# Attention, index and scan heads two at a time on the two halves of the matmul array, their GpSimd work on VectorE, and modulation sums in two column halves

## Chip, core and metric

The kernel runs on one core of one Trainium2 chip. The metric is the device time of one execution in microseconds (us). TensorE (PE) multiplies; its array has 128 rows (the partitions that are contracted) and 128 columns (the partitions of the result in PSUM). VectorE (DVE), ScalarE (ACT) and GpSimd (POOL) do the element-wise work, and SyncE (SP) issues most transfers. Every engine works through its own queue in order.

## What is computed

The program is two transformer-like blocks on 512 tokens of width 1024. The change touches the first block's mixer: an attention that keeps the best 128 keys of each query by an index score, a state-space scan in chunks of 128 tokens, and the modulation vectors.

```python
mod = cond @ w_ada + b_ada                       # six vectors of 1024
sh_m, sc_m, g_m, sh_f, sc_f, g_f = jnp.split(mod, 6)
h = _rms(x, norm_mix) * (1 + sc_m) + sh_m
q, kv_lat, q_i, k_i, w_i, z, xbc, dt_raw, gate_logits = _split(h @ w_in)
# index, per query q, 8 heads of 64
dots = jnp.einsum('bqhd,bsd->bqhs', q_i, k_i)
score = jnp.einsum('bqh,bqhs->bqs', w_i, jax.nn.relu(dots))   # causal; top 128 kept
# attention, 8 heads of 64
logits = q . k * scale + bias(dist);  p = softmax(logits);  y = p @ v
# scan, 16 heads of 64, state 128, chunks of 128
wmat = cb[..., None] * lmat * dtc
y = wmat @ xc + (cc @ state) * exp(acum)
state = state * exp(acum[-1]) + (decay * xc)^T @ bc
```

After it come the mixer's output products, a mixture of 32 experts (about 400 MB of weights), and the second block. None of these is touched.

## The kernel before

The mixer has one long stream of large products: `proj` (from L524) takes a group of 256 columns of `w_in`, splits the weights into a high part H (`nc.scalar.copy`, L368) and a low part L (a subtraction, L370: seven of eight on VectorE, one on GpSimd), and multiplies three times per block (`mm3`, L387 to L389, 512 columns each). There are 2 groups for the queries, the key and value products, and then 18 groups in `ssm`.

Everything else of the mixer is written as Python generators. After each step of `proj` the function `pace` advances two lists by the rates of the tables `RATES` and `R0`: `bg` (index `scores`, then `qknorm`, `steps`, `heads`, and `ssd` once its inputs are there) and `bg2` (`topk` for three query blocks, then `modrest`, the four modulation vectors that are needed late). So small matmuls stand between large ones in PE's queue; what is left when the groups end is drained.

- `scores` (L628): for a query block t (1 to 3) and each of 8 heads one matmul that contracts 64 rows, then ReLU on ACT and a weighted sum on DVE.
- `heads` (L780 to L859): 32 units, one for a query block t (0 to 3) and a head h. `weights` multiplies q and k of the head (L813, 64 rows: the lower half of the array for even heads, the upper for odd, up to 512 columns), adds mask and bias and takes the maximum on DVE (L817, L819), takes exp on ACT (L824), and normalises on DVE (L826, L827). `turn` transposes the result, block by block (L835), and ACT copies it (L837). `output` multiplies with v (L847, 64 columns of the array, the half given by the head; t + 1 matmuls). In step i the unit i is weighed, i - 1 turned and i - 2 multiplied. `bias` (L796, 8 calls) is on GpSimd.
- `ssd` (L1172 to L1281): four chunks. `weights` prepares four heads at a time (L1212, L1215 on DVE, exp on ACT, and the product L1221 on GpSimd); `output` multiplies, head by head, L1234 and (from the second chunk) L1236, both in the column half of the head; `post` scales on GpSimd (L1253, L1258) and updates the state (L1261).
- `modrest` (L1303 to L1338): sums eight weighted rows on DVE (L1318), then one matmul with a single column of ones per half of 512 (L1324), a copy, a DMA, and for two of the vectors four tiny matmuls per half (L1336).

float32 operands pass through the array twice, so each such matmul is two records in the trace ("x2" is one matmul of a head); the transposes are one. PSUM tiles come from two rings of four banks, "mm" for large products and "at" for the rest.

Of the kernel before, what the change touches and what calls it, by code (L numbers as in the profile page):

```python
# [18 lines left out]
P = 128  # L19
# [143 lines left out]
R0 = (2.5, 1), (3, 0.75), (2, 1.25)  # L163
RATES = ([1.35, 1.35, 1.125, 1.125, 1.125, 1.125, 1.125, 1.125, 1.35, 1.125, 1.125, 1.125, 1.125, 1.125, 1.125, 0.9, 0.9, 0.45],
# [102 lines left out]
class Kern:  # L267
# [352 lines left out]
    def scores(self, qiT, kiT, wi):  # L620
        nc, c = self.nc, self.c
        for t in range(1, NT):
            n = (t + 1) * P
            sc = self.pt([P, n], f"score{t}")
            for h in range(8):
                r0 = 64 * (h % 2)
                b = self.bank()
                nc.tensor.matmul(b[:, :n], lhsT=qiT[r0:r0 + 64, h // 2, t * P:(t + 1) * P], rhs=kiT[r0:r0 + 64, :n], start=True, stop=True)  # L628
                rl = self.w2()
                nc.scalar.activation(rl[:, :n], b[:, :n], AF.Relu)  # L630
                if h == 0:
                    nc.vector.tensor_scalar(sc, rl[:, :n], wi[:, t, :1], 0.0, op0=OP.mult, op1=OP.add)
                else:
                    nc.vector.scalar_tensor_tensor(sc, rl[:, :n], wi[:, t, h:h + 1], sc, op0=OP.mult, op1=OP.add)
                if h == 7:
# [144 lines left out]
    def heads(self):  # L780

        nc, c = self.nc, self.c
        qT, kT, V, T = self.qT, self.kT, self.V, self.T
        units = [(t, h) for t in range(NT) for h in range(8)]
# [7 lines left out]
        def bias(t, hq):  # L792
# [3 lines left out]
            nc.gpsimd.tensor_tensor(mb[:, :, :near], T[:, 4 * hq:4 * hq + 4, 256 - near:],  # L796
# [3 lines left out]
        def weights(t, h):  # L800
# [3 lines left out]
            if h % 4 == 0:  # L804
                nt, nq = (t, 1) if h == 0 else (t + 1, 0)
                if (t, h // 4) not in mbs:
                    bias(t, h // 4)
                if nt < NT:
                    bias(nt, nq)
            mb = mbs[t, h // 4]  # L810
            r0 = 64 * (h % 2)
            b = self.bank()
            nc.tensor.matmul(b[:, :n], lhsT=qT[r0:r0 + 64, h // 2, t * P:n], rhs=kT[r0:r0 + 64, h // 2, :n], start=True, stop=True)  # L813
            lg = self.w2()
            mx = self.small([P, 2])
            if far:
                nc.vector.tensor_tensor_reduce(out=lg[:, :far], in0=b[:, :far], in1=mask(t)[:, :far], scale=1.0,  # L817
                                               scalar=-3.0e38, op0=OP.add, op1=OP.max, accum_out=mx[:, 1:])
            nc.vector.tensor_tensor_reduce(out=lg[:, far:n], in0=b[:, far:n], in1=mb[:, h % 4, :near], scale=1.0,  # L819
                                           scalar=mx[:, 1:] if far else -3.0e38, op0=OP.add, op1=OP.max, accum_out=mx[:, :1])  # L820
            nm = self.small([P, 1])
            nc.vector.tensor_scalar(nm, mx[:, :1], -1.0, None, op0=OP.mult)
            ss = self.small([P, 1])
            nc.scalar.activation(lg[:, :n], lg[:, :n], AF.Exp, bias=nm, accum_out=ss)  # L824
            rs = self.small([P, 1])
            nc.vector.reciprocal(rs, ss)  # L826
            nc.vector.tensor_scalar(lg[:, :n], lg[:, :n], rs, None, op0=OP.mult)  # L827
            st[t, h] = lg

        def turn(t, h):  # L830
            n = (t + 1) * P
            lg = st[t, h]
            pb = self.bank()
            for k in range(t + 1):
                nc.tensor.transpose(pb[:, k * P:(k + 1) * P], lg[:, k * P:(k + 1) * P], c("ident"))  # L835
            pt = self.w2()
            nc.scalar.copy(pt[:, :n], pb[:, :n])  # L837
            st[t, h] = pt

        def output(t, h):  # L840
            pt = st.pop((t, h))
            if h % 2 == 0:
                st["y"] = self.bank()
            yb = st["y"]
            r0 = 64 * (h % 2)
            for k in range(t + 1):
                nc.tensor.matmul(yb[r0:r0 + 64, :P], lhsT=V[:, k, h * 64:(h + 1) * 64], rhs=pt[:, k * P:(k + 1) * P], start=k == 0, stop=k == t)  # L847
            if h % 2:
                nc.scalar.copy(self.yat[:, h // 2, t * P:(t + 1) * P], yb[:, :P])

        for i in range(len(units) + 2):
# [3 lines left out]
            if 0 < i <= len(units):  # L855
# [316 lines left out]
    def ssd(self):  # L1172
# [31 lines left out]
        def weights(ch, hq):  # L1204
# [12 lines left out]
            if ch:  # L1217
# [3 lines left out]
                nc.gpsimd.tensor_tensor(e3, e3, BC[:, 2 + g, None, cs].to_broadcast([P, 4, P]), op=OP.mult)  # L1221
# [4 lines left out]
        def output(ch, hq):  # L1226
# [4 lines left out]
            for h in range(4):  # L1231
                o = yb[64 * (h % 2):64 * (h % 2) + 64, (h // 2) * P:(h // 2 + 1) * P]
                H = hq * 4 + h
                nc.tensor.matmul(o, lhsT=xdt[:, H], rhs=w[:, h * P:(h + 1) * P], start=True, stop=ch == 0)  # L1234
# [1227 lines left out]
```

## Time and profile before

| | |
|---|---|
| median of 3 runs | 2329.55 us (2326.49 to 2334.56) |
| profiled execution, its own time | 2326.67 us |
| its span, first to last instruction | 2324.9 us |
| PE busy | 2199.6 us (95%) |
| VectorE busy | 1518.0 us (65%) |
| ScalarE busy | 982.2 us (42%) |
| GpSimd busy | 291.5 us (13%) |
| granted TensorE clock | 0.981 |

Shares over the span mix stages with different limits. The mixer's products with the work between them lie from about 60 to 490 us; experts follow to about 1640 us, and the second block after that. A record's printed length for PE is modelled; what a matmul costs is read from the distance of the starts around it.

### The profile page before, as it was taken

The page shows a single profiled execution, that of the slowest core. Times are in us where ns is not written, and L with a number is a line of the kernel's source. Part 1 is how long each engine was busy: PE and PEld are TensorE (multiplying, and loading weights), DVE is VectorE, ACT ScalarE, POOL GpSimd, SP SyncE. Part 2 cuts the span into 40 slices and gives each one's busy share as a digit, 9 for nine tenths or more (in the row PEclk, how much of TensorE's full clock was granted, in tenths as well). Part 3 has the DMA queues.
Part 4 walks back from the last instruction along what each step waited for, and adds up shares of the span by engine and source line. Part 5 has one row for each costly group of instructions (what it writes and reads, how often), then busy time and mean ns, then how long its engine had stood idle before and what let it go on. Part 6 is the DMA issues. An engine that isn't in the chain of part 4 may idle for free. (4 is left out here: it accounts for less than half of the span.)

```text
span 2324.9 us, 28001 instructions
## 1 busy us (share of the span) xinstructions
PE 2199.6 (95%) x10209; PEld 1576.0 (68%) x10209; DVE 1518.0 (65%) x2480; ACT 982.2 (42%) x1375; POOL 291.5 (13%) x173
## 2 busy tenths in 40 slices
PE   6999999999899999999999999999799999999898
PEld 4676667678666657655656666666368888888676
DVE  7678878864776668766667667776442534458864
ACT  4424443432444446534345445544233422336642
POOL 2011101421111100110010010000000111002110
PEclk9999999999899999999999999999989999999999
DMA  8323344652889999999999999999732222132221
GB/s 313 99 94 107 122 150 173 231 205 115 313 339 398 407 405 411 398 411 397 395 397 398 397 397 379 405 404 408 300 110 91 91 91 91 73 109 87 77 91 37
DMA packets 93938, 576.36 MB, mean 248 GB/s; under 512 B 12591, under 2 KB 14361, under 8 KB 32611
## 3 DMA queue, kind: packets, MB, share of 16 engines
q1 hardware_dynamic: 79856, 540.60, 59.4%
q0 software_dynamic: 8432, 18.21, 3.1%
q10 hardware_dynamic: 5508, 15.71, 1.8%
q8 instruction: 82, 1.34, 0.2%
q14 instruction: 60, 0.49, 0.1%
HBM read 556.74 MB, written 27.59 MB: 251 GB/s over the span
## 5 line engine op out<-in xcount | busy, mean ns | idle before, releaser
L370 DVE TENSOR_TENSOR L<-raw,H 128x1024 fp32r<-128x1024 f32 x476 | 582.5, 1257 | 258.1 <-ACT H L368 245.8
L368 ACT CAST H<-raw 128x1024 fp32r<-128x1024 f32 x496 | 508.8, 1051 | 473.8 <-DMA raw<-in_w_dn_dram 148.0
L388 PE MATMUL mm<-L,hl 128*128 128x512 f32 x536 | 211.2, 394 | 5.1 <-DVE L L370 5.1
L387 PE MATMUL mm<-H,hl 128*128 128x512 f32 x536 | 211.5, 395 | 1.3 <-ACT H L368 1.3
L389 PE MATMUL mm<-H,hl 128*128 128x512 f32 x536 | 209.5, 391 | 0.0
L387 PE MATMUL mm<-U,H 128*128 128x512 f32 (+1 forms) x488 | 187.6, 384 | 3.0 <-DVE U L710 3.0
L389 PE MATMUL mm<-U,L 128*128 128x512 f32 (+1 forms) x488 | 185.2, 381 | 1.1 <-POOL L L370 1.1
L388 PE MATMUL mm<-U,H 128*128 128x512 f32 (+1 forms) x488 | 186.2, 382 | 0.0
L1674 PE MATMUL mm<-raw,sx 128*64 128x512 f32 x792 | 179.3, 598 | 0.0
L387 PE MATMUL mm<-E,H 128*128 128x512 f32 x416 | 172.8, 418 | 3.9 <-ACT E L393 3.9
L387 PE MATMUL mm<-H,U 128*128 128x512 f32 x424 | 169.8, 401 | 2.1 <-DVE w L2361 2.0
L389 PE MATMUL mm<-H,U 128*128 128x512 f32 x424 | 167.8, 396 | 0.0
L388 PE MATMUL mm<-E,H 128*128 128x512 f32 x416 | 165.7, 398 | 1.6 <-DVE E L394 1.6
L388 PE MATMUL mm<-L,U 128*128 128x512 f32 x424 | 167.1, 394 | 0.0
L389 PE MATMUL mm<-E,L 128*128 128x512 f32 x416 | 165.2, 397 | 0.0
L388 PE MATMUL at<-L,hl 128*128 128x512 f32 x272 | 111.1, 408 | 18.8 <-DVE L L370 18.7
L388 PEld LDWEIGHTS mm<-L,hl 128*128 128x128 f32 x536 | 100.7, 188 | 32.2 <-DVE L L370 12.1
L1674 PEld LDWEIGHTS mm<-raw,sx 128*64 128x64 f32 x792 | 53.9, 137 | 98.5 <-issue 92.7
L387 PE MATMUL at<-H,hl 128*128 128x512 f32 x272 | 108.8, 400 | 11.5 <-ACT H L368 11.5
L387 PEld LDWEIGHTS mm<-H,hl 128*128 128x128 f32 x536 | 100.9, 188 | 22.7 <-ACT H L368 1.7
L389 PEld LDWEIGHTS mm<-H,hl 128*128 128x128 f32 x536 | 100.6, 188 | 20.8
L387 PEld LDWEIGHTS mm<-U,H 128*128 128x128 f32 x488 | 92.7, 190 | 22.1 <-DVE U L710 3.1
(452 smaller groups left out, 3731.4 us busy)
## 6 DMA issues: line engine op xcount, KB each, us to landing
raw<-in_w_gu_dram SPq DMA_DIRECT2D x212, 1024.0 KB
raw<-in_w_dn_dram SPq DMA_DIRECT2D x103, 1024.0 KB
XU<-in_w_gu_dram SPq DMA_DIRECT2D x44, 1024.0 KB
XU<-in_w_dn_dram SPq DMA_DIRECT2D x25, 1024.0 KB
raw<-in_win_dram SPq DMA_DIRECT2D x20, 1024.0 KB
raw<-in_w_ada_dram SPq DMA_DIRECT2D x16, 1024.0 KB
raw<-in_wug_dram SPq DMA_DIRECT2D x16, 1024.0 KB
raw<-in_wxg_dram SPq DMA_DIRECT2D x12, 1024.0 KB
```

The source lines that it names most:

```text
L368: nc.scalar.copy(h[:, :m], src)
L370: eng.tensor_tensor(l[:, :m], src, h[:, :m].bitcast(F32), op=OP.subtract)
L387: t.matmul(out, lhsT=lhs[0], rhs=rhs[0], start=start, stop=False)
L388: t.matmul(out, lhsT=lhs[0], rhs=rhs[1], start=False, stop=False)
L389: t.matmul(out, lhsT=lhs[1], rhs=rhs[0], start=False, stop=stop)
L1674: nc.tensor.matmul(bs[i // 2][64 * (i % 2):64 * (i % 2) + 64], lhsT=x[:, k], rhs=w[:, i * 512:(i + 1) * 512], start=False, stop=k == KD - 1)
```

## The change

1. `scores`, `heads` and `ssd.output` issue two heads' matmuls next to each other: QK of an even and an odd head (row halves), PV alternating between the two heads (column halves), the scan's matmuls alternating. `heads` has 16 units of two heads; `output` now follows the `turn` of the same unit, and `turn` copies back into the tile that it read.
2. 25 element-wise operations move from GpSimd to VectorE: `bias` (8), the scan's product with C (12), and the two scalings in `post` (3 and 2).
3. `modrest` multiplies with 64 columns of ones for each half of 512, one in the lower, one in the upper column half; the tiny matmuls of both halves follow after a yield, in one bank with one copy.
4. `RATES` and `R0` are about halved where heads run in pairs.

```diff
-R0 = (2.5, 1), (3, 0.75), (2, 1.25)
-RATES = ([1.35, 1.35, 1.125, 1.125, 1.125, 1.125, 1.125, 1.125, 1.35, 1.125, ...
+R0 = (1.25, 1), (1.5, 0.75), (1, 1.25)
+RATES = ([1.35, 1.35, 0.7, 0.6, 0.6, 0.6, 0.6, 0.6, 0.65, 0.6, 0.6, 0.6, 0.7, 1.125, ...
...
-            nc.gpsimd.tensor_tensor(mb[:, :, :near], T[:, 4 * hq:4 * hq + 4, 256 - near:],
+            nc.vector.tensor_tensor(mb[:, :, :near], T[:, 4 * hq:4 * hq + 4, 256 - near:],
...
+            bs = [self.bank() for _ in range(2)]
+            for i in range(2):
+                r0 = 64 * i
+                nc.tensor.matmul(bs[i][:, :n], lhsT=qT[r0:r0 + 64, h0 // 2, t * P:n], rhs=kT[r0:r0 + 64, h0 // 2, :n], start=True, stop=True)
...
+            for lg in st[t, h0]:
+                pb = self.bank()
+                for k in range(t + 1):
+                    nc.tensor.transpose(pb[:, k * P:(k + 1) * P], lg[:, k * P:(k + 1) * P], c("ident"))
+                nc.scalar.copy(lg[:, :n], pb[:, :n])
...
+            yb = self.bank()
             for k in range(t + 1):
+                for i, pt in enumerate(pts):
+                    nc.tensor.matmul(yb[64 * i:64 * i + 64, :P], lhsT=V[:, k, (h0 + i) * 64:(h0 + i + 1) * 64], rhs=pt[:, k * P:(k + 1) * P], start=k == 0, stop=k == t)
...
-            if i > 1:
-                output(*units[i - 2])
+                output(*units[i - 1])
                 yield
...
-                nc.gpsimd.tensor_tensor(e3, e3, BC[:, 2 + g, None, cs].to_broadcast([P, 4, P]), op=OP.mult)
+                nc.vector.tensor_tensor(e3, e3, BC[:, 2 + g, None, cs].to_broadcast([P, 4, P]), op=OP.mult)
...
+                for last in (False, True) if ch else (False,):
+                    for i in (h, h + 1):
+                        o = yb[64 * (i % 2):64 * (i % 2) + 64, (i // 2) * P:(i // 2 + 1) * P]
...
-            nc.gpsimd.tensor_tensor(xdt, xdt, dec[:, :, None].to_broadcast([P, 16, 64]), op=OP.mult)
+            nc.vector.tensor_tensor(xdt, xdt, dec[:, :, None].to_broadcast([P, 16, 64]), op=OP.mult)
...
-                nc.gpsimd.tensor_tensor(s3, s3, ea[:, :, None].to_broadcast([P, 16, 64]), op=OP.mult)
+                nc.vector.tensor_tensor(s3, s3, ea[:, :, None].to_broadcast([P, 16, 64]), op=OP.mult)
...
+            b = self.bank()
             for h in range(2):
+                nc.tensor.matmul(b[64 * h:64 * h + 64], lhsT=c("ones")[:, :64], rhs=acc[:, h * 512:(h + 1) * 512], start=True, stop=True)
```

How this stands in the queues, at three places. First PE, in the heads of the last query block, before the change: one head's PV (L847, four matmuls into one column half), six products, the next head's QK (L813). Names are out<-in, the last figure the shape of the result.

```order
L389 MATMUL mm_2584<-E_68,L_2580 128x512
L847 MATMUL at_2686<-w_650_2684,XU_937 64x128 x4
L387 MATMUL mm_2765<-E_67,H_2757 128x512
L388 MATMUL mm_2765<-E_69,H_2757 128x512
L389 MATMUL mm_2765<-E_67,L_2758 128x512
L387 MATMUL mm_2766<-E_67,H_2757 128x512
L388 MATMUL mm_2766<-E_69,H_2757 128x512
L389 MATMUL mm_2766<-E_67,L_2758 128x512
L813 MATMUL at_2773<-U_882,U_578 128x512
L387 MATMUL mm_2765<-E_67,H_2757 128x512
```

The same engine and place after the change, first the QK of two heads (L818), then the transposes of two heads (L845), the products behind them, and PV (L853).

```order
L388 MATMUL mm_2571<-E_69,H_2562 128x512
L389 MATMUL mm_2571<-E_67,L_2563 128x512
L818 MATMUL at_2588<-U_882,U_578 128x512
L818 MATMUL at_2589<-U_882,U_578 128x512
L387 MATMUL mm_2570<-E_67,H_2562 128x512
L388 MATMUL mm_2570<-E_69,H_2562 128x512
L389 MATMUL mm_2570<-E_67,L_2563 128x512
```

The two QK rows stand next to each other, in two banks. A little further on in the same queue come the transposes of the pair before and its PV.

```order
L845 MATMUL at_2630<-cst_66,w_583_2486 128x128 x4
L845 MATMUL at_2636<-cst_66,w_587_2494 128x128 x4
L387 MATMUL mm_2570<-E_68,H_2566 128x512
L388 MATMUL mm_2570<-E_70,H_2566 128x512
L389 MATMUL mm_2570<-E_68,L_2567 128x512
L387 MATMUL mm_2571<-E_68,H_2566 128x512
L388 MATMUL mm_2571<-E_70,H_2566 128x512
L389 MATMUL mm_2571<-E_68,L_2567 128x512
L853 MATMUL at_2648<-w_583_2486,XU_937 64x128
L387 MATMUL mm_2570<-E_68,H_2566 128x512
L853 MATMUL at_2648<-w_587_2494,XU_937 64x128
L853 MATMUL at_2648<-w_583_2486,XU_937 64x128
```

PV alternates between the two heads' tiles, and six products stand between the last transpose and the first PV matmul, where the copy by ACT has to be done. In the whole stream 32 single QK rows have become 16 pairs, and all 16 PV groups alternate. In the index scores the rows stand in the same order as before.

Third place: VectorE in the scan. Before, its queue holds the weights (L1212, L1215), the low parts (L370), the sums of `modrest` (L1318) and the outputs (L1240), while L1221, L1253 and L1258 stand in GpSimd's queue.

```order
L1264 TENSOR_TENSOR state_2942<-state_2942,at_3395 128x512
L1264 TENSOR_TENSOR state_2942<-state_2942,at_3398 128x512
L1215 TENSOR_TENSOR w_795_3443<-w_795_3443,cb_3309 128x512
L1318 SCALAR_TENSOR_TENSOR macc_3095<-raw_3560,cond_84,macc_3095 128x1024
L1240 SCALAR_TENSOR_TENSOR U_990<-U_990,prm_72,at_3426 128x128 x2
L1212 TENSOR_SCALAR w_798_3477<-raw_3174,ac_1305 128x128 x4
L370 TENSOR_TENSOR L_3524<-raw_3517,H_3523 128x1024
L1215 TENSOR_TENSOR w_798_3477<-w_798_3477,cb_3309 128x512
L1240 SCALAR_TENSOR_TENSOR U_990<-U_990,prm_72,at_3460 128x128 x2
L1212 TENSOR_SCALAR w_816_3570<-raw_3407,ac_1305 128x128 x4
L1318 SCALAR_TENSOR_TENSOR macc_3095<-raw_3586,cond_84,macc_3095 128x1024 x2
```

After, the scaling (L1259) and the products with C (L1225) stand between them.

```order
L1216 TENSOR_SCALAR w_706_3099<-raw_2930,ac_1311 128x128 x4
L1227 COPY s_696_3045<-raw_2930 128x4
L1216 TENSOR_SCALAR w_709_3133<-raw_2930,ac_1311 128x128 x3
L1246 SCALAR_TENSOR_TENSOR U_991<-U_991,prm_72,at_3069 128x128 x2
L1259 TENSOR_TENSOR w_669_2892<-w_669_2892,s_702_3087 128x1024
L1219 TENSOR_TENSOR w_706_3099<-w_706_3099,cb_3030 128x512
L1225 TENSOR_TENSOR w_707_3106<-w_707_3106,U_989 128x512
L1216 TENSOR_SCALAR w_709_3133<-raw_2930,ac_1311 128x128
L1225 TENSOR_TENSOR w_710_3140<-w_710_3140,U_989 128x512
L1272 COPY state_2886<-at_3091 128x512
L1272 COPY state_2886<-at_3094 128x512
```

From the output product of the attention onwards (after the groups of `ssm`), every engine's queue is the same as before, row for row.

## Rows read from the trace of the kernel before

**Rows 1.** Windows: us, then busy us (records) of PE, PEld, DVE, ACT, POOL; clock, DMA share, GB/s.

```profile
165.00:340.00 175.00, 173.46 (x755) 117.10 (x754) 135.96 (x317) 71.33 (x156) 24.59 (x11) 1.00 0.36 124
400.00:450.00 50.00, 45.63 (x282) 35.31 (x281) 46.82 (x83) 19.90 (x33) 25.33 (x14) 1.00 0.63 223
700.00:1600.00 900.00, 868.97 (x4000) 557.40 (x3999) 624.18 (x827) 420.32 (x476) 81.90 (x54) 1.00 1.01 400
```

**Rows 2.** Timeline of PE in the heads: start, us, engine, line, operation.

```profile
174.15 0.48 PE L813 MATMUL at<-U,U 64*128 64x128 f32 x2
174.57 0.50 PE L387 MATMUL mm<-E,H 128*128 128x512 f32 x1
...
347.12 1.09 PE L847 MATMUL at<-w,XU 128*64 128x128 f32 x8
348.13 0.50 PE L387 MATMUL mm<-E,H 128*128 128x512 f32 x1
...
349.17 0.39 PE L388 MATMUL mm<-E,H 128*128 128x512 f32 x1
349.40 0.40 PE L389 MATMUL mm<-E,L 128*128 128x512 f32 x1
349.72 1.12 PE L813 MATMUL at<-U,U 64*128 64x512 f32 x2
350.78 0.50 PE L387 MATMUL mm<-E,H 128*128 128x512 f32 x1
```

**Rows 3.** Timeline of PE, index scores: twelve heads and the next product.

```profile
102.65 3.48 PE L628 MATMUL at<-w,U 64*128 64x384 f32 x12
106.33 3.59 PE L628 MATMUL at<-w,U 64*128 64x512 f32 x12 [0.20 <-ACT w L630]
109.85 0.50 PE L388 MATMUL mm<-E,H 128*128 128x512 f32 x1
```

**Rows 4.** Timeline of PE, first chunk of the scan: four heads.

```profile
382.87 0.66 PE L1234 MATMUL at<-w,w 128*64 128x128 f32 x8
383.45 0.50 PE L388 MATMUL mm<-E,H 128*128 128x512 f32 x1
```

**Rows 5.** Timeline of PE, a modulation sum and the next product.

```profile
329.79 1.02 PE L1324 MATMUL at<-macc,cst 128*1 128x512 f32 x2
330.74 0.50 PE L388 MATMUL mm<-E,H 128*128 128x512 f32 x1
```

**Rows 6.** GpSimd's groups, 160 to 470 us: busy, mean ns, idle before.

```profile
L1221 POOL TENSOR_TENSOR w<-w,U 128x512 f32<-128x512 f32 x12 | 18.5, 1554 | 42.0 <-ACT w L1219 42.0
L796 POOL TENSOR_TENSOR w<-XU,score 128x1024 f32<-128x1024 f32 x6 | 15.6, 2614 | 63.9 <-DMA gate<-w 24.0 <-DVE s L819 15.2 <-DVE score L650 13.7
L1253 POOL TENSOR_TENSOR w<-w,s 128x1024 f32<-128x1024 f32 x3 | 6.9, 2312 | 4.0 <-PE at L1236 2.7 <-DVE w L1212 1.3
```

**Rows 7.** VectorE in the scan: groups (busy, mean ns); then by line, ns min/median/max.

```profile
L1212 DVE TENSOR_SCALAR w<-raw,ac 128x128 f32<-128x128 f32 x64 | 24.3, 441 | 1.5 <-PE at L1236 1.5
L1215 DVE TENSOR_TENSOR w<-w,cb 128x512 f32<-128x512 f32 x16 | 14.8, 935 | 0.8 <-ACT w L1213 0.8
...
L1212 DVE TENSOR_SCALAR w<-raw,ac x64: 273/279/1943, 361.1 to 458.1; 128x128 f32<-128x128 f32 x64
L1215 DVE TENSOR_TENSOR w<-w,cb x16: 679/686/1811, 369.6 to 459.4; 128x512 f32<-128x512 f32 x16
L370 DVE TENSOR_TENSOR L<-raw,H x476: 1202/1221/4811, 66.3 to 2289.8; 128x1024 fp32r<-128x1024 f32 x159
```

**Rows 8.** ScalarE's groups, 165 to 470 us: busy, mean ns, idle before.

```profile
L368 ACT CAST H<-raw 128x1024 fp32r<-128x1024 f32 x34 | 35.4, 1046 | 37.2 <-PE mm L388 28.2 <-DMA raw<-in_win_dram 4.9 <-DMA raw<-in_wao_dram 4.1
L837 ACT COPY w<-at 128x512 f32<-128x512 f32 x8 | 4.7, 586 | 15.6 <-PE at L835 13.3 <-DMA raw<-in_w_ada_dram 2.3
```

**Rows 9.** Waits of VectorE and PE: total us, times, longest us.

```profile
DVE s L826 <- ACT w L824: 20.4, 19, 3.1
...
PE at L1261 <- ACT bt L1249: 3.4, 1, 3.4
```

More of the change, by code (lines that the diff above doesn't have):

```diff
@@ L783, in heads @@
         qT, kT, V, T = self.qT, self.kT, self.V, self.T
-        units = [(t, h) for t in range(NT) for h in range(8)]
+        units = [(t, h) for t in range(NT) for h in range(0, 8, 2)]
         mbs, st = {}, {}
@@ L803, in weights @@
             far = n - near
[L804 to L807, printed above, removed]
+            if h0 % 4 == 0:
+                nt, nq = (t, 1) if h0 == 0 else (t + 1, 0)
+                if (t, h0 // 4) not in mbs:
+                    bias(t, h0 // 4)
                 if nt < NT:
                     bias(nt, nq)
-            mb = mbs[t, h // 4]
-            r0 = 64 * (h % 2)
-            b = self.bank()
@@ L813, in weights @@
[L813 to L830, printed above, removed]
-            n = (t + 1) * P
-            lg = st[t, h]
-            pb = self.bank()
-            for k in range(t + 1):
[L835 to L851, printed above, removed]
+            mb = mbs[t, h0 // 4]
@@ new lines, in weights @@
+            bs = [self.bank() for _ in range(2)]
+            for i in range(2):
+                r0 = 64 * i
+                nc.tensor.matmul(bs[i][:, :n], lhsT=qT[r0:r0 + 64, h0 // 2, t * P:n], rhs=kT[r0:r0 + 64, h0 // 2, :n], start=True, stop=True)
+            lgs = []
+            for i in range(2):
+                h, b = h0 + i, bs[i]
+                lg = self.w2()
+                mx = self.small([P, 2])
+                if far:
+                    nc.vector.tensor_tensor_reduce(out=lg[:, :far], in0=b[:, :far], in1=mask(t)[:, :far], scale=1.0,
+                                                   scalar=-3.0e38, op0=OP.add, op1=OP.max, accum_out=mx[:, 1:])
+                nc.vector.tensor_tensor_reduce(out=lg[:, far:n], in0=b[:, far:n], in1=mb[:, h % 4, :near], scale=1.0,
+                                               scalar=mx[:, 1:] if far else -3.0e38, op0=OP.add, op1=OP.max, accum_out=mx[:, :1])
+                nm = self.small([P, 1])
+                nc.vector.tensor_scalar(nm, mx[:, :1], -1.0, None, op0=OP.mult)
+                ss = self.small([P, 1])
+                nc.scalar.activation(lg[:, :n], lg[:, :n], AF.Exp, bias=nm, accum_out=ss)
+                lgs.append((lg, ss))
@@ new lines, in weights, with turn @@
+            for lg, ss in lgs:
+                rs = self.small([P, 1])
+                nc.vector.reciprocal(rs, ss)
+                nc.vector.tensor_scalar(lg[:, :n], lg[:, :n], rs, None, op0=OP.mult)
+            st[t, h0] = [lg for lg, _ in lgs]
+        def turn(t, h0):
+            n = (t + 1) * P
+            for lg in st[t, h0]:
[3 more added lines that the diff above has]
+                nc.scalar.copy(lg[:, :n], pb[:, :n])
@@ L852, in heads, with output @@
+        def output(t, h0):
+            pts = st.pop((t, h0))
+            yb = self.bank()
+            for k in range(t + 1):
+                for i, pt in enumerate(pts):
+                    nc.tensor.matmul(yb[64 * i:64 * i + 64, :P], lhsT=V[:, k, (h0 + i) * 64:(h0 + i + 1) * 64], rhs=pt[:, k * P:(k + 1) * P], start=k == 0, stop=k == t)
+            nc.scalar.copy(self.yat[:, h0 // 2, t * P:(t + 1) * P], yb[:, :P])
+        for i in range(len(units) + 1):
             if i < len(units):
@@ L1230, in output @@
             yb = self.bank()
[L1231 to L1234, printed above, removed]
-                if ch:
-                    nc.tensor.matmul(o, lhsT=St[:, H * 64:(H + 1) * 64], rhs=ea[:, h * P:(h + 1) * P], start=False, stop=True)
+            for h in range(0, 4, 2):
+                for last in (False, True) if ch else (False,):
+                    for i in (h, h + 1):
+                        o = yb[64 * (i % 2):64 * (i % 2) + 64, (i // 2) * P:(i // 2 + 1) * P]
+                        H = hq * 4 + i
+                        a, b = (St[:, H * 64:(H + 1) * 64], ea) if last else (xdt[:, H], w)
+                        nc.tensor.matmul(o, lhsT=a, rhs=b[:, i * P:(i + 1) * P], start=not last, stop=last or ch == 0)
             for f in range(2):
```

58 lines of the change are left out of this document (29 added, 29 removed).

## The prediction

> **What bounds the kernel now.** I read the windows by stage first, then PE's timeline inside the stage, then the other engines' groups and waits. In the heads' stage, 165 to 340 us, PE is busy 173.5 of 175 us and VectorE 136.0 [rows 1]: PE ends last, and VectorE is at 78%. In the scan, 400 to 450 us, it is closer: PE 45.6 and VectorE 46.8 of 50 us [rows 1]; there PE waits, once 3.4 us for a copy before the state update [rows 9]. After that the experts load at a DMA share of 1.01 [rows 1], and there transfers set the time. The change's rows end before that stage, and behind the mixer every queue is the same row for row, so time gained by the mixer is passed on if the loads of the experts start earlier by as much. They do, as far as I can see: in the heads the DMA share is 0.36 [rows 1], so no transfer holds the mixer, and those loads wait for buffers that the mixer frees. TensorE's granted clock is 1.00 in both mixer windows [rows 1], its upper level of 2.4 GHz, and it stayed there with PE idle for 4.4 of 50 us; I count nothing for the clock.
>
> **QK in pairs.** A single head costs PE from its start to the start of the next product, plus its entry. For 512 columns that is 350.78 - 349.72 = 1.06 us, and the entry is the 0.32 us from the last product's start to it, less the 0.23 us that products are apart, 0.09: together 1.15 us [rows 2]. For 128 columns it is 0.42 + 0.09 = 0.51 us [rows 2]. The four widths come eight times each, in equal steps: 32 x (0.51 + 1.15) / 2 = 26.6 us. Do two row halves overlap? Index scores show it: there twelve heads, four of 384 and eight of 512 columns, stand in a row, and take 109.85 - 102.65 = 7.2 us with 0.2 us of waiting [rows 3]. Singly, by the step above (384 columns: 0.94), they would take 4 x 0.94 + 8 x 1.15 = 13.0 us. So a pair costs about what one costs, and QK falls by half: **-13.3 us**. For the index scores themselves I count nothing, since their rows already stood side by side in the queue before.
>
> **PV in pairs.** One head's four matmuls into one column half take 348.13 - 347.12 = 1.01 us, with entry 1.10 [rows 2]. Four matmuls that alternate between the halves, in the first chunk of the scan, take 383.45 - 382.87 = 0.58 us [rows 4]: that is two steps instead of four, so a step is (1.01 - 0.58) / 2 = 0.215 us and one block costs 1.10 - 3 x 0.215 = 0.455 us. Over one to four blocks the mean is 0.78 us; 32 heads make 24.9 us, half of it goes: **-12.4 us**. The bounds of this are 0 (no overlap) and 12.4; I take the upper one because rows 4 show overlap for the same shape. The scan's own alternation gains little: its first chunk is unchanged, and from the second chunk on an even and an odd head's matmuls already touch different halves in turn. I count 0, at most 1 us. The 80 transposes stay and stand in larger groups: 0, within 1 us.
>
> **Modulation sums.** A matmul of 512 columns takes 330.74 - 329.79 = 0.95 us [rows 5], eight of them 7.6 us. With 64 columns each and in two column halves they overlap as PV does: **-3.8 us**. The tiny matmuls stay as many. Their results are needed long after.
>
> PE's part is thus -13.3 - 12.4 - 3.8 = **-29.5 us**. It counts in full only while PE ends last, and two new waits speak against that.
>
> **GpSimd's work on VectorE.** Moved are twelve products of 512 columns, as long as VectorE's own L1215 (median 686 ns [rows 7]), 8.2 us; eleven operations of 1024 columns, as long as L370 there (1221 ns [rows 7]), 13.4 us; and two of 512, 1.4 us: +23.0 us. GpSimd needed 18.5 + 15.6 + 6.9 = 41.0 us for most of them [rows 6]. While GpSimd works, VectorE's operations stretch: L1212 has a median of 279 ns, a maximum of 1943 and a mean of 441, and L1215 a median of 686 and a mean of 935 [rows 7]. So 64 x 0.162 + 16 x 0.249 = 14.4 us come back in the scan, about what the scan gets (8.2 us and five wide operations, 6.1 us). In the heads VectorE gets 8.7 us, and gets back between 0 and that. The Trainium skill (SBUF — State Buffer, Who interferes with whom) has the reason: a GpSimd instruction that reads SBUF and a VectorE instruction with two SBUF inputs, or in a two-port mode, exclude each other for a whole instruction. By that alone as much as the 41 us could come back, and VectorE would end 18 us lighter; L1212's stretched ones agree in kind, while the means bear out only 14.4 us.
>
> What does VectorE's load do to PE? If the heads' stage shrinks from 175 by some 25 us to 150, VectorE has 136 to 145 us to do in it: 91 to 96%. The nearest row for such a load is the scan, VectorE 94% busy and PE idle for 4.4 of 50 us, 8.7% [rows 1]; at that rate the stage loses 14 us. The other end is 0, since the heads' chain waits less in pairs: before, VectorE stood 20.4 us, 19 times, for the exp before the reciprocal [rows 9], and now the second head's reductions stand in between. I take **+4 us**, nearer to 0, because part of the scan's idle time is the 3.4 us wait for one copy.
>
> **PV right behind the turn.** Before, a whole unit lay between a head's transposes and its PV; now often six products do (two to twelve), 6 x 0.23 = 1.4 us [rows 2], and PV has ACT's copies queued ahead of it. The first copy runs beside the second head's transposes; the second takes 0.59 us [rows 8] after them, or with the first still ahead 1.17, and if a cast of 1.05 us [rows 8] stands in ACT's queue, 2.2 us. So PE waits between 0 and 0.8 us at each of 16 units, 0 to 13 us, and the next products are queued behind that matmul. I take **+4 us**: narrower units copy less, and ACT is busy 71 of 175 us [rows 1].
>
> **The sum.** -29.5 + 4 + 4 = -21.5 us. Against the profiled execution's own 2326.67 us that is 2305.2; that execution lies 2.9 us below the median of the three runs, so I forecast the median at 2329.55 - 21.5 = **2308.0 us**.
>
> **Rivals.**
> 1. *All of it arrives.* ACT and VectorE keep up, and the scan's 4.4 us of PE idle time [rows 1] goes as well, since no GpSimd step is left in its chain: -34 us, 2295.5. For it speaks that VectorE's total hardly grows; against it, the load of 91 to 96%.
> 2. *VectorE becomes the bound of the heads.* The 14 us are lost, and 8 of the 13 us at PV: -29.5 + 22 = -7.5 us, 2322. The Trainium skill (TensorEngine Tiling (Array Packing), PSUM Bottleneck) warns of this: tiling speeds up the matmuls, not the reading of PSUM, which may become the bound. Rows 1 bear it out in the scan only.
> 3. *Slower: the shorter pipeline of the heads.* A pair's chain is longer than a head's (two QK, four reductions, two exp, then two reciprocals), and with 16 units instead of 32, and PV one tick behind the turn, fewer units are in flight. If PE waits at each turn for the mean 1.1 us of that exp wait (20.4 / 19 [rows 9]), 17 us, and for 0.8 us at each PV, 13 us, and loses the 14 us, then it is -29.5 + 44 = +14.5 us, 2344. It turns slower when a unit's waits pass 29.5 / 16 = 1.84 us on average.
> 4. *The pairs don't pair.* The second QK of a pair waits for its own bank, and PE works in order; if the first has ended by then, nothing overlaps, and only half of the 64 entries of 0.09 us go (2.9 us) while the 8 us of waits come: +5 us, 2335.
>
> **Chances.** Forecast 0.52, rival 1 0.20, rival 2 0.18, rival 3 0.06, rival 4 0.04. The forecast's own spread is 15 to 28 us of gain (2301 to 2315). About 0.3%, 7 us, is what a measurement of this kernel can tell from no change. Faster by more: the forecast, rival 1 and half of rival 2, 0.81. Within: the other half and rival 4, 0.13. Slower: rival 3, 0.06. The range takes in rival 1 and nearly all of rival 2: 2294 to 2324; what is left out is rivals 3 and 4 and the outer edges of the others, less than 2 in 10.
>
> **What would show it.** PE's timeline: two QK records of a pair starting within some ns of each other, the pair taking 1.1 us at 512 columns; eight PV matmuls at four blocks taking about 1.0 us. Windows: the heads' stage some 20 us shorter, VectorE over 90% busy in it, the scan's L1212 back at a mean near 280 ns. Waits of PE: for L837 before PV and for L827 before the transposes, each a few us; if they reach 10 us each, rival 2 has it, and near 20 us each rival 3. Behind the mixer everything should be shifted by the same amount; if the experts' stage starts earlier but ends where it did, my step from the mixer to the end is wrong. The forecast falls if the pairs' starts lie a whole matmul apart, or if VectorE's busy time in the mixer grows by the full 23 us.

## The result, and the profile after

The changed kernel takes 2303.35 us (median of 4 runs, 2300.28 to 2304.66), against 2328.02 us for the kernel before in the same series (2325.99 to 2334.56): a ratio of 0.9886, 95% interval 0.9873 to 0.9899, 24.7 us less. The forecast was 2308.0, within 2294 to 2324. Medians here and below are of runs in the fast state; two runs of the kernel before in a later series, 3126 and 3638 us at granted clocks of 0.65 and 0.56, are left out.

| us | before | after |
|---|---|---|
| span of the profiled execution | 2324.9 | 2298.5 |
| first matmul of the index scores to first of L950 (after: L954) | 381.6 | 355.6 |
| from there to the end | 1854.3 | 1853.1 |
| VectorE busy | 1518.0 | 1515.9 |
| GpSimd busy | 291.5 | 247.9 |

L950 is the first matmul of the short step that follows the `ssm` groups. The second row of the table is called the mixer's length from here on; it holds 26.0 of the span's 26.4 us. Behind it, where the queues are the same, the profiles of all the kernels here lie between 1853.1 and 1859.4 us, so a few us between two medians can also come from there; each experiment below is therefore read by both.

The mixer as one window, before and after, columns as in rows 1:

```profile
89.04:470.63 381.59, 368.66 (x1788) 260.90 (x1788) 311.80 (x697) 153.98 (x301) 68.01 (x36) 0.99 0.42 145
89.77:445.38 355.61, 342.35 (x1788) 251.61 (x1788) 309.73 (x720) 154.17 (x301) 24.76 (x11) 0.98 0.44 156
```

PE's busy time fell by 26.3 us and its idle time, the rest of the window, rose by 0.3 (12.93 to 13.26): the gain is matmul time, and PE's waits changed places without changing much in sum.

In the kernel after, L813 has become L818 (QK), L826/L827 L836/L837 (normalising), L835 L845 (transposes), L847 L853 (PV), L796 L800 (bias), L1212/L1215/L1221/L1234 L1216/L1219/L1225/L1242 (scan), L1318/L1324 L1324/L1330 (modulation sums).

The windows of rows 1, of the kernel after:

```profile
165.00:340.00 175.00, 174.53 (x897) 127.30 (x896) 154.73 (x373) 83.95 (x179) 9.30 (x5) 1.00 0.42 151
400.00:450.00 50.00, 41.49 (x238) 32.23 (x237) 36.95 (x63) 16.02 (x25) 8.15 (x2) 0.89 0.72 270
700.00:1600.00 900.00, 872.12 (x3997) 567.64 (x3994) 633.76 (x826) 428.25 (x481) 81.14 (x54) 0.99 1.01 401
```

In the heads PE is still the engine that ends last (174.5 of 175 us), now with 897 records for 755; VectorE has gone from 136.0 to 154.7 us, 88%, and GpSimd from 24.6 to 9.3. In 400 to 450 us, which now holds the end of the scan and the drain behind the groups, PE is worse off than before: 41.5 us for 45.6, at a granted clock of 0.89. The experts' stage runs at a DMA share of 1.01 as before.

PE's timeline after: a QK pair of 128 and one of 512 columns with the product behind each, one PV of four blocks, one modulation sum, and the scan's first four heads (answers to rows 2, 4 and 5; x4 is two matmuls):

```profile
175.35 0.49 PE L818 MATMUL at<-U,U 64*128 64x128 f32 x4
175.77 0.50 PE L387 MATMUL mm<-E,H 128*128 128x512 f32 x1
...
309.70 1.08 PE L1330 MATMUL at<-macc,cst 128*64 128x512 f32 x4
310.71 0.50 PE L387 MATMUL mm<-E,H 128*128 128x512 f32 x1
312.31 1.13 PE L818 MATMUL at<-U,U 64*128 64x512 f32 x4
313.38 0.50 PE L387 MATMUL mm<-E,H 128*128 128x512 f32 x1
...
320.66 1.09 PE L853 MATMUL at<-w,XU 128*64 128x128 f32 x16
321.68 0.50 PE L387 MATMUL mm<-E,H 128*128 128x512 f32 x1
...
340.35 0.66 PE L1242 MATMUL at<-w,w 128*64 128x128 f32 x8
340.94 0.50 PE L387 MATMUL mm<-E,H 128*128 128x512 f32 x1
```

The two matmuls of a pair start 0 to 10 ns apart in 15 of the 16 pairs (in the sixteenth, PV matmuls stand between the two, which start at 266.89 and 268.53 us, so not every pair stands together as the section on the change has it), and a pair of 512 columns costs 313.38 - 312.31 = 1.07 us where one head cost 1.06 [rows 2]. PV of both heads takes 1.02 us where one took 1.01 [rows 2]. The sums' two halves take 1.01 us where each took 0.95 [rows 5].

VectorE by line (ns min/median/max, first and last start), answering rows 6 and 7:

```profile
L800 DVE TENSOR_TENSOR w<-XU,score x6: 1216/1218/1224, 167.4 to 260.7; 128x1024 f32<-128x1024 f32 x6
L1216 DVE TENSOR_SCALAR w<-raw,ac x64: 268/281/290, 332.4 to 419.3; 128x128 f32<-128x128 f32 x64
L1219 DVE TENSOR_TENSOR w<-w,cb x16: 673/682/687, 338.6 to 421.2; 128x512 f32<-128x512 f32 x16
```

L1212's maximum of 1943 ns and L1215's of 1811 [rows 7] have become 290 and 687, and the bias takes 1.22 us on VectorE for 2.61 on GpSimd [rows 6].

The waits of PE in the mixer (total us, times, longest us), answering rows 9:

```profile
PE mm L389 <- DVE L L370: 4.2, 1, 4.2
PE at L1242 <- DVE w L1219: 3.2, 1, 3.2
PE mm L387 <- DVE U L713: 3.0, 1, 3.0
...
PE at L845 <- DVE w L837: 0.5, 1, 0.5
```

And the wait of VectorE that rows 9 began with:

```profile
DVE s L836 <- ACT w L832: 2.3, 4, 1.0
```

The wait of 20.4 us for the exp [rows 9] is down to 2.3: the second head's reductions fill it. The wait of the transposes for the normalising (L837; L827 before), which the prediction put at a few us, is 0.5, and there is none of PV for ScalarE's copy. L713's 3.0 us lie ahead of the heads and were there before (for L710). The two largest, 4.2 and 3.2 us, lie at the end of the scan. VectorE's timeline there:

```profile
422.42 1.28 DVE L1324 SCALAR_TENSOR_TENSOR macc<-raw,cond,macc 128x1024 f32<-128x1024 f32 x1
...
426.48 1.28 DVE L1324 SCALAR_TENSOR_TENSOR macc<-raw,cond,macc 128x1024 f32<-128x1024 f32 x1
427.67 4.29 DVE L946 SCALAR_TENSOR_TENSOR U<-w,U 128x512 f32<-128x512 f32 x7
431.89 2.35 DVE L370 TENSOR_TENSOR L<-raw,H 128x1024 fp32r<-128x1024 f32 x2
```

The last modulation sums (L1324, 1.28 us each) stand among the scan's work, then seven operations of L946, then the low part (L370) for which PE waits until 433.15. The wait also costs clock, as the window shows:

```profile
420.00:440.00 20.00, 12.71 (x45) 9.00 (x46) 15.60 (x21) 9.45 (x15) 8.15 (x2) 0.74 0.88 337
```

Behind those two waits 15 of the products between 424.6 and 438.9 us stand 0.43 us apart rather than 0.23, as at TensorE's lower level of 1.2 GHz: 15 x 0.2 = 3 us.

### The profile page after: what moved, and what is told of

Read it like the earlier page. It is cut to its first block, busy times and chain, and to the rows that moved or that the text cites. A ratio compares the mean times of both kernels' runs of the same rounds, so it can differ in the third digit from the quotient of the medians.

```text
span 2298.5 us, 27983 instructions
## 1 busy us (share of the span) xinstructions
PE 2176.4 (95%) x10209; PEld 1569.7 (68%) x10209; DVE 1515.9 (66%) x2503; ACT 982.5 (43%) x1375; POOL 247.9 (11%) x148
## 5 line engine op out<-in xcount | busy, mean ns | idle before, releaser
L370 DVE TENSOR_TENSOR L<-raw,H 128x1024 fp32r<-128x1024 f32 x476 | 578.4, 1248 | 258.2 <-ACT H L368 245.7
L368 ACT CAST H<-raw 128x1024 fp32r<-128x1024 f32 x496 | 509.1, 1051 | 475.6 <-PE mm L389 146.0
L387 PE MATMUL at<-H,hl 128*128 128x512 f32 x272 | 109.4, 402 | 10.4 <-ACT H L368 10.2
L389 PE MATMUL at<-H,hl 128*128 128x512 f32 x272 | 108.7, 400 | 0.0
```

The lines of the kernel that those rows point to most:

```text
L368: nc.scalar.copy(h[:, :m], src)
L370: eng.tensor_tensor(l[:, :m], src, h[:, :m].bitcast(F32), op=OP.subtract)
L387: t.matmul(out, lhsT=lhs[0], rhs=rhs[0], start=start, stop=False)
L389: t.matmul(out, lhsT=lhs[1], rhs=rhs[0], start=False, stop=stop)
```

## The experiments

All twelve kernels are edits of the kernel after, but for two that edit the kernel before. Each was timed together with new runs of the kernel before, its own series. The differences are of medians, each within its own series: after is 24.7 us below before. Ratios are against the kernel before, with 95% intervals.

**Does the pairing of QK bring its 13 us?** A yield between the two QK puts products between them; the heads' shares of the first stream are raised by a third, since there is a step more:

```
+                if i == 0:
+                    yield
```

> The changed kernel, but the two QK matmuls of a pair are set apart by one step of the background work, so that six large products stand between nearly all of them; the rates of the heads are raised by a third, since a unit now has four steps instead of three. Theory (overlap on the two row halves): QK costs single again, 13 us more, time about 2316. Rival A (VectorE freed of GpSimd): no change, 2303. Rival B (fewer breaks): some 16 breaks of 0.1 us each come back, 1.5 us, 2305.

2318.84 us, 0.9954 [0.9941, 0.9968]: 13 us less of the gain by the difference (11.4 for 24.7), and the mixer is 15.2 us longer. Of these, 12.3 are PE's busy time (354.7 us for 342.4), 2.9 its idle time; so most of the loss is the matmuls themselves and not waits that the raised shares could bring. The theory holds.

**Does the pairing of PV, and which part of it?** First the two heads' PV one head after the other, in place of alternating block by block, but still side by side:

```
-            for k in range(t + 1):
-                for i, pt in enumerate(pts):
+            for i, pt in enumerate(pts):
+                for k in range(t + 1):
```

> The changed kernel, but PV of a pair is issued head after head (all blocks of the even head, then all of the odd one) instead of alternating. Same matmuls, same places in the queue, same operations on the other engines. Theory (what was gained is that two heads' matmuls run at the same time on two halves of the array): the 16 PV groups of four blocks go from about 1.1 us back to about 2.0 us, PE gets 11 to 12.5 us longer, and the time is about 2314 us, 11 us above the changed kernel. Rival A (what was gained is VectorE freed of GpSimd): no change within 2 us, 2303. Rival B (halved rates and fewer breaks in the stream of products): no change either, 2303.

2303.73 us, 0.9892 [0.9877, 0.9907]: no change that the intervals could tell. The theory's 11 us did not come, because the edit did not undo the overlap. PE's timeline, the PV that took 1.02 us above:

```profile
320.85 1.58 PE L853 MATMUL at<-w,XU 128*64 128x128 f32 x16
322.36 0.50 PE L387 MATMUL mm<-E,H 128*128 128x512 f32 x1
```

1.51 us: less than two heads singly (2 x 1.01), more than alternating. What alternation gains here is small in sum: groups of one and two blocks take the same in either order (0.37 and 0.59 us), products stand within part of the longer alternating groups, and the mixer is only 0.8 us longer. Then the two heads apart, with a yield between them and the shares raised as above:

```
+            for i, pt in enumerate(pts):
+                if i:
+                    yield
+                for k in range(t + 1):
```

> The changed kernel, but the PV matmuls of a pair's two heads are set apart by one step, so that large products stand between them; the heads' rates are raised by a third, as in the run with QK apart. In the run with PV head after head four blocks took 1.60 us for both heads, against 1.12 alternating and 2.23 for two single heads, and the mixer grew by less than 1 us. Theory (heads next to each other overlap, in whatever order): PV apart costs single again, 10 to 13 us more than the changed kernel, 2314 to 2317. Rival (PV is not what PE's time hangs on, so its overlap gains nothing): within 2 us of the changed kernel, 2301 to 2306.

2313.74 us, 0.9934 [0.992, 0.9949], 10.4 us less of the gain, mixer 10.1 us longer, all of it PE's busy time (353.1 us for 342.4; idle 12.6 for 13.3): the theory holds, and what counts is that the two heads stand side by side.

**The sums.** The old `modrest`, with one column of ones for each half:

> The changed kernel with the modulation sums as before: one column of ones, one half after the other, no extra step. Theory: PE gets 3.6 us longer for the sums; against that the background list has four steps fewer, so the last vector's weighted sums on VectorE come earlier, and the waits of PE in the drain behind the groups (3.2 us for L1219, 4.2 and 1.0 us for what stands behind the sums in VectorE's queue) may shrink: between 2303 and 2307. If overlap in the sums were nothing, the time would fall by what the drain gives back, 2298 to 2303.

2306.31 us, 0.9904 [0.9889, 0.9919]: 24.0 us below its own series, which is 0.7 less than the kernel after and can't be told from nothing; the mixer is 2.7 us longer, against 3.8 predicted. By the mixer the term holds about in size.

**The move from GpSimd.** All 25 operations back on GpSimd, the pairs kept:

```
-            nc.vector.tensor_tensor(mb[:, :, :near], T[...
+            nc.gpsimd.tensor_tensor(mb[:, :, :near], T[...
...
-                nc.vector.tensor_tensor(e3, e3, ...
+                nc.gpsimd.tensor_tensor(e3, e3, ...
```

> The changed kernel with the 25 element-wise operations put back on GpSimd; pairs and sums as changed. Theory (PE's overlapped matmuls are the gain, VectorE is a condition for it): VectorE's operations stretch again by 20 to 28 us beside GpSimd, while 23 us of its own go, so its load hardly changes; the scan's chain waits for GpSimd as before: 2 to 8 us above the changed kernel, 2305 to 2311. Rival A (VectorE freed is the main gain): 15 us or more above, 2318 or more.

2318.82 us, 0.9956 [0.9943, 0.997], mixer 11.2 us longer: 13.2 us of gain lost. More than the theory allowed, and about what rival A named. And the other corner, the kernel before with nothing but the move:

> The kernel before with nothing changed but the 25 operations moved from GpSimd to VectorE. The run with them back on GpSimd came out 11 us longer in the mixer, with PE waiting 7.3 us for VectorE before the transposes. Theory (moving them is a condition that matters when PE's work shrinks; with single heads PE is 99% busy in the heads and hardly waits): between 0 and 5 us faster than before, from the scan's waits, 2325 to 2330 against 2330. Rival (the move is worth its 11 to 15 us by itself): 2315 to 2319.

2324.6 us, 0.9988 [0.9978, 0.9997], 3.4 us less: the move by itself is worth little, and rival A falls with it. So everything else, with the operations left on GpSimd, gains 11.4, the move alone 3.4, both 24.7: some 10 us exist only when both are made. Where? The eight bias operations alone back on GpSimd:

> The changed kernel with the 8 bias operations of the heads alone back on GpSimd; the scan's 17 stay on VectorE. If the 11 us of the run with all 25 back come from the heads (VectorE held up there while GpSimd works, so that PE waits before the transposes), 6 to 9 us above the changed kernel, 2309 to 2312. If they come from the scan, within 2 us, 2301 to 2306.

2314.99 us, 0.9942 [0.9928, 0.9956], mixer 12.6 us longer (PE idle 9.9 us more, and busy 2.7 us more at a granted clock of 0.97 for 0.98): 11.7 us of gain lost by the medians, most of what all 25 lose (13.2). The wait of PE that grew:

```profile
PE at L845 <- DVE w L837: 8.9, 6, 4.1
```

GpSimd's timeline ahead of the longest of these six waits:

```profile
262.28 5.72 POOL L800 TENSOR_TENSOR w<-XU,score 128x1024 f32<-128x1024 f32 x2 [13.64 <-DVE score L653]
```

VectorE's timeline at the same place:

```profile
262.77 2.97 DVE L370 TENSOR_TENSOR L<-raw,H 128x1024 fp32r<-128x1024 f32 x1
265.67 2.88 DVE L892 SCALAR_TENSOR_TENSOR U<-w,U 128x512 f32<-128x512 f32 x1
268.48 0.28 DVE L825 CUSTOM_DVE_ANT_0 w<-at,score 128x128 f32<-128x128 f32 x1
```

A wait that took 0.5 us in the kernel after takes 8.9 here. Two bias operations run on GpSimd from 262.28 to 268.0; beside them VectorE's L370 takes 2.97 us for 1.22 [rows 7], L892 2.88 (0.67 to 0.69 in eleven of twelve in the kernel after). The reduction L825 reads the score and not the bias; it stands behind the two in VectorE's queue and starts at 268.48 without an idle time of VectorE before it; PE then stands 4.1 us before the transposes, about what the two were stretched by (3.9). At a shorter wait it is the normalising itself that is stretched:

```profile
210.40 2.35 POOL L800 TENSOR_TENSOR w<-XU,score 128x1024 f32<-128x1024 f32 x1 [19.68 <-DVE s L836]
210.80 2.03 DVE L837 TENSOR_SCALAR w<-w,s 128x128 f32<-128x128 f32 x1
212.89 0.33 PE L845 MATMUL at<-cst,w 128*128 128x128 f32 x1 [1.98 <-DVE w L837]
```

The same operation takes 0.26 us at 191.26, with GpSimd idle. Five of the six waits, 8.0 of the 8.9 us, follow a bias operation in this way, and VectorE never waits for GpSimd in this mixer: not a late bias but VectorE stretched beside it makes PE wait. The heads have no slack for that: in 150 to 345 us PE is busy 184.6 us here and 194.5 in the kernel after. With single heads PE waited little at this place:

```profile
PE at L835 <- DVE w L827: 1.4, 3, 0.6
```

The scan's 17 operations alone:

> The changed kernel with the scan's moved element-wise operations (L1225, L1259, L1264) on GpSimd again and the eight bias operations of the heads left on VectorE. Theory (the loss of 15 us with all of them on GpSimd lies in the bias operations, which alone cost 11 us): within 2 us of the changed kernel, 2301 to 2305. Rival (each part alone costs, and the two hide one another): 5 to 10 us more, 2308 to 2313.

2306.9 us, 0.9902 [0.9887, 0.9917], mixer 2.3 us longer: 2.9 us of gain lost, between the theory (within 2) and the rival (5 or more). By the medians the two parts, 11.7 and 2.9, add up to 14.6 for the 13.2 of all 25; by the mixer, 12.6 and 2.3 for 11.2. Two of PE's waits that are new here ("issue": the profile names nothing that PE waited for):

```profile
PE at L1267 <- issue: 3.6, 1, 3.6
...
PE at L1242 <- POOL w L1225: 2.5, 1, 2.5
```

They stand in place of others: PE's idle time in the mixer is 12.7 us, for 13.3 in the kernel after. What grew is its busy time, 345.2 us for 342.4, at a granted clock of 0.97 for 0.98.

**The shares.** The tables of the kernel before, in the kernel after:

```
-R0 = (1.25, 1), (1.5, 0.75), (1, 1.25)
-RATES = ([1.35, 1.35, 0.7, 0.6, 0.6, ...
+R0 = (2.5, 1), (3, 0.75), (2, 1.25)
+RATES = ([1.35, 1.35, 1.125, 1.125, 1.125, ...
```

> The changed kernel with the shares of the old table (the first entry of the three early pairs 2.5, 3 and 2 in place of 1.25, 1.5 and 1; the heads 1.125 to 1.35 in place of 0.6 to 0.7), so that a pair of heads is asked to advance about twice as fast beside the other streams. Theory (the new shares matter: at the old ones the heads' products, their softmax on ScalarE and the normalising on VectorE crowd together, and TensorE waits for L837 before the transposes and for the copies before PV): 5 to 15 us more than the changed kernel, 2308 to 2318. Rival (the shares only set which fill stands where; the sum of VectorE's and TensorE's work is the same): within 2 us, 2301 to 2305.

2324.96 us, 0.9986 [0.9977, 0.9995]: 21 of 24.7 us are gone, more than either expected. ScalarE's timeline at the longest wait of PE:

```profile
244.41 0.59 ACT L900 ACTIVATE w<-mm 128x512 f32<-128x512 f32 x1
254.92 0.61 ACT L832 ACTIVATE w<-w,s 128x384 f32<-128x384 f32 x1 [9.92 <-DVE s L830]
255.53 0.57 ACT L900 ACTIVATE w<-mm 128x512 f32<-128x512 f32 x1
```

PE's timeline, the product that waits:

```profile
256.16 0.80 PE L387 MATMUL mm<-E,H 128*128 128x512 f32 x1 [10.14 <-ACT w L900]
```

And the window around it, columns as in rows 1:

```profile
240.00:260.00 20.00, 8.09 (x32) 4.78 (x32) 19.15 (x50) 4.16 (x10) 0.00 (x0) 0.74 0.07 26
```

From 243 to 254 VectorE works off a row of top-k steps (L650, L651, 0.7 us each), with the heads' reduction behind them in its queue. ScalarE stands 9.9 us at the exp (L832) that needs it, and behind that exp stands the gate (L900) that empties the bank for the next product: PE stands 10.1 us. Right behind the row, at 254.86, comes the bias that needs its result, and the kernel's function `mask`, which the bias calls, drives the top-k list on until that block is done: heads that run ahead would put just such a row into VectorE's queue. That this call did it is read from the code, not shown. Further waits (3.5 for L1219, 1.8 and 1.6 for L368) follow at 328 to 365 us; the mixer is 16.4 us longer, 11.6 of it PE's idle time, and the rest of the 21 us lies behind it and isn't assigned. The size was missed, the theory's kind of wait is there, in another place: not transposes or PV, but products, through ScalarE.

**The drain.** The late sums can be brought forward or thinned. Two yields fewer in `modrest` (the one behind the two halves stays only for the two vectors that have tiny matmuls):

> The changed kernel without the two extra steps of the modulation list that do nothing (for the first and the last vector, which have no tiny matmuls). Its list then ends two steps earlier; the weighted sums of the last vector stand less deep in the drain. If what PE waits for there (3.2 and 4.2 us behind VectorE's sums) is caused by these late sums, 1 to 5 us are gained, 2298 to 2302; if the waits come from the scan's own chain, nothing changes, 2303.

2305.23 us, 0.9902 [0.9888, 0.9916], mixer 2.7 us longer; the wait for L370 grew from 4.2 to 8.6 us. No gain. Then the shares of the second stream:

```
-          [..., 0.55, 0.55, 0.4, 0.25, 0.25, 0, 0, 0.4])
+          [..., 0.55, 0.55, 0.55, 0.4, 0.4, 0.1, 0, 0.4])
```

> The changed kernel with the second stream's shares raised at the indices 12 to 15 (0.55, 0.4, 0.4, 0.1 in place of 0.4, 0.25, 0.25, 0), so that the last modulation sums lie among the heads and not in the drain behind them, where TensorE waited about 8 us in the changed kernel for VectorE (L370 4.2, L1219 3.2, L713 3.0). Theory (those waits come from the sums' VectorE work, L1324, queued ahead of what TensorE wants): 3 to 7 us less than the changed kernel, 2296 to 2300. Rival (the drain is a chain of its own, as when two useless yields were taken away and the wait for L370 grew to 8.6 us): within 2 us or up to 3 us more, 2301 to 2306.

2296.46 us (2295.96 to 2298.75), 0.9861 [0.9846, 0.9876]: the fastest kernel here, 32.2 us below before, 7.5 more than the kernel after gains; the mixer is 7.8 us shorter (PE idle 4.5 us less, and busy 3.2 us less at a granted clock of 1.00 for 0.98). Two of PE's waits in it:

```profile
PE mm L389 <- DVE L L370: 1.5, 2, 0.9
PE at L1242 <- DVE w L1219: 1.3, 1, 1.3
```

And its window from 420 to 440 us:

```profile
420.00:440.00 20.00, 20.00 (x137) 14.92 (x137) 19.36 (x35) 12.31 (x19) 5.68 (x2) 1.00 0.71 253
```

The waits of 4.2 and 3.2 us are 1.5 and 1.3, and PE is busy all of 420 to 440 us at full clock. Is that a gain of the earlier sums alone? The same edit in the kernel before:

> The kernel before with the same raise of the second stream's shares (0.55, 0.4, 0.4, 0.1 in place of 0.4, 0.25, 0.25, 0 at the indices 12 to 15) that took 6.9 us off the changed kernel. Theory (the changed kernel's loss behind the groups is its own: there VectorE, with 23 us more of work, still had sums to do when the groups ended; in the kernel before TensorE's waits in the drain are 3.4 us for a copy by ScalarE and 1.9 us for the scan's state, none for VectorE's low parts or weights): within 3 us of the kernel before, 2325 to 2331. Rival (late sums cost the kernel before as much, and the earlier pace is a gain of its own): 5 to 8 us less, 2320 to 2323.

2344.32 us, 1.0066 [1.0052, 1.008]: 15.8 us slower than before, which neither expected; the mixer is 10.2 us longer, and the profile 4.1 us behind it. Two of its waits of PE:

```profile
PE at L1234 <- DVE w L1215: 3.4, 2, 3.0
...
PE mm L389 <- DVE L L370: 2.6, 1, 2.6
```

And the window in which the longest of them lies, first in the kernel before, then here:

```profile
400.00:420.00 20.00, 20.00 (x123) 14.98 (x122) 17.61 (x38) 9.02 (x17) 14.25 (x8) 1.00 0.47 162
400.00:420.00 20.00, 16.13 (x90) 12.89 (x91) 20.00 (x36) 8.63 (x14) 9.55 (x6) 0.91 0.52 188
```

With the sums earlier, VectorE is busy all 20 us from 400 to 420 for 17.6, in the scan, and PE, which had no idle time there, waits for the weights (3.0 us at 405.1) and ahead of it, at 382.8, for L370: what it waits for in the drain of the kernel after. So the edit fits the kernel after and not the one before. Which part of the kernel before makes the difference was not tried.

## Why the prediction was right, and where its steps were off

- **PE's part, -29.5.** Right in sum and part by part. Read from the starts as in the prediction, QK gives -13.2 (predicted -13.3), PV -12.3 (-12.4), the sums -3.6 (-3.8). Taking each part out costs 15.2, 10.1 and 2.7 us of the mixer. PE's busy time in the mixer fell by 26.3 us, which is these 29 less the 3 us of lower clock. Counting nothing for the index scores was right as well: in the kernel after the twelve heads of rows 3 take 110.57 - 103.37 = 7.2 us again. Rival 4 (the pairs don't pair) falls with the starts 0 to 10 ns apart in 15 of 16. The scan's alternation, counted as 0, was not taken out by itself; its first chunk takes 0.59 us for 0.58.
- **VectorE's busy time.** The prediction moved 23.0 us to VectorE and let 14.4 us come back in the scan, up to 8.7 more in the heads. VectorE's busy time fell by 2.1 us in all, so about 25 us came back, a little over the upper bound drawn from the rows (23.1); the "full 23 us" that would have made the forecast fall did not stay. The 41 us that the prediction took as possible by the Trainium skill's rule (SBUF — State Buffer, Who interferes with whom) were not reached; the stretched L370 and L892 beside GpSimd, 2.97 and 2.88 us, agree with the rule in kind.
- **+4 for VectorE's load in the heads.** Mis-sized, and in the wrong place. At 88% load (the "over 90%" was nearly met) PE waited there 0.5 us. VectorE held PE up at the end instead: 7.4 us of waits for L370 and L1219, and 3 us of lower clock. The step read the 4.4 idle us of rows 1 as a price of load. They were two single waits, 1.9 us for the scan's state and, up to 450 us, 2.5 of the 3.4 us for ScalarE's copy: the price of particular things standing in a queue. The kernel with the sums earlier, with hardly less work on VectorE (308.4 us in the mixer for 309.7), takes most of the new waits away.
- **+4 for PV behind the turn.** Too much: PE's waits show none of PV for the copy (L846). Only PV's weight loads (PEld, which overlap PE's work) wait for it, 2.8 us in 8 times against 1.4 us in 4 before: a cost of 1.4 us at most.
- **The clock, 0.** The prediction argued that the clock stayed up although PE stood for 4.4 of 50 us. But that window of rows 1 ends at 450 us, while the wait of 3.4 us in it ends at 450.9. The next 6 us of the kernel before read otherwise, as the last section shows. The clock is part of a wait's price, in both kernels.
- **The sum.** The forecast was +8 for new waits in the heads. New waits of some 7 us came at the end of the scan, with 3 us of lower clock, but about as much of the old waits went, the 3.4 us before the state update among them, which the prediction had left standing (only its rival 1 let them go). By the mixer the +8 measure about +3.5: 0.3 of idle time and 3 of clock. So the mixer gained 26.0 us for the 21.5 forecast, and the medians 24.7. The number came near by the right size of PE's part; that the rest did little harm is in part luck.
- **What the move is worth.** Here a step was missing. The prediction asked what the moved work costs VectorE, and let the return be a matter of VectorE's busy time. That the heads in pairs could not have kept their gain with the bias on GpSimd, 11 to 13 us, was in none of its terms. Busy time hardly shows it (VectorE 1519.3 us with all 25 back, 1515.9 without); it shows in which operations of VectorE are stretched and in PE's wait behind them.
- **The shares.** The prediction named no price for the new tables; it took them as a part of the pairing. Nearly the whole gain hangs on them: with the old ones the ratio is 0.9986. That the forecast held here is luck: the new ones were in the kernel, and it had not looked.
- **Rivals 2 and 3.** Rival 2 (VectorE the bound of the heads) did not come in this kernel. Its wait shows in another one: with the bias on GpSimd PE waits 8.9 us for L837 before the transposes, near the 10 us that it named. That wait came from stretched operations; no run here separates reading PSUM from VectorE's other work. Rival 3's waits did not come: the exp wait fell from 20.4 to 2.3 us, where it had been expected at each turn.
- **Passing on.** Behind the mixer all moved by the same amount (1854.3 and 1853.1 us), as the prediction took it.

## What to carry to other kernels

Two independent matmuls on two halves of the array cost PE what one costs (here 1.07 us for 1.06, and 1.02 for 1.01), if they stand next to each other in its queue; read it from the starts, and expect the sum of these savings only while the other engines' queues keep time. When a stage is made denser, look for work that holds up another engine while it runs and that only the old slack hid (here a bias on GpSimd, beside which single operations of VectorE took about 1.8 to 2.2 us more), and re-time the streams: a table of shares can hold nearly the whole gain. A wait costs where something stands in a queue ahead of what is wanted, so moving late work earlier can pay more than taking work away, but only in the kernel for which it was timed.

## Not expected of the hardware

Two heads' matmuls into the two column halves overlap even when one head's four stand wholly before the other's: 1.51 us for both, between 1.02 (alternating) and 2.02 (two singly). The single records of the group at 320.85 fit two rows of starts 0.11 us apart, the second beginning at 321.34, ahead of the last three of the first. That would make the second head begin before the first is through; the profile doesn't name a record's head, so it isn't settled.

Behind two of PE's longer waits the granted clock is lower in the kernel before, too. Its windows behind the waits for L710 (3.0 us, ended at 116.9), for the copy of rows 9 (3.4, ended at 450.9) and for the scan's state (1.9, ended at 421.8):

```profile
117.00:130.00 13.00, 12.92 (x48) 10.03 (x49) 12.59 (x36) 6.72 (x13) 0.00 (x0) 0.87 0.24 81
450.00:456.00 6.00, 5.11 (x31) 3.23 (x33) 3.72 (x7) 1.38 (x4) 0.00 (x0) 0.72 0.44 156
421.00:428.00 7.00, 6.15 (x47) 4.85 (x48) 7.00 (x15) 2.95 (x4) 1.82 (x2) 1.00 0.42 142
```

The granted clock is 0.87 and 0.72 behind the two longer waits and 1.00 behind the shorter. A window that ends with a wait does not show what it cost. Whether the length of a wait alone decides is not shown.
